# Planning the landing of every transfer a fifth later in a list scheduler

## The chip, the core and the metric

One core of a Trainium2 chip runs the whole program. The metric is the device time of one execution in microseconds (us). PE is TensorE (matrix products), DVE is VectorE, ACT is ScalarE, POOL is GpSimd, SP is SyncE, which here only issues transfers (DMAs). Each engine works through its own instructions in their order; an instruction that needs another engine's result waits on a semaphore, and all behind it on its engine wait too.

## The reference

A decoder trunk of two layers on 1024 tokens of width 1024, all in fp32. The first layer mixes tokens by a causal convolution, the second by sliding-window attention; an MLP with a squared ReLU and a gated embedding (p) follow in each.

```
def conformer_conv(x, w_in, b_in, w_dw, b_dw, ln_g, ln_b, w_out, b_out):
    a, gate = jnp.split(x @ w_in + b_in, 2, axis=-1)
    h = a * jax.nn.sigmoid(gate)
    h = causal_depthwise_conv(h, w_dw, width=31) + b_dw
    h = jax.nn.silu(layer_norm(h, ln_g, ln_b))
    return h @ w_out + b_out

for i in range(2):
    y = conformer_conv(x, ...) if i == 0 else swa_sink_attention(x, ...)   # window 128, 16 heads, 4 kv heads
    x = layer_norm(ALPHA * x + y)
    x = layer_norm(ALPHA * x + square(relu(x @ w_up)) @ w_down)
    x = x + (p[i] @ ple_w_proj[i]) * sigmoid(x @ ple_w_gate[i])
```

## The kernel before

Every fp32 product is made of three products on PE: operands are split in a high part and the rest (tiles xh and xl for activations, wh and wl for weights), and xh\*wh, xl\*wh and xh\*wl are summed in PSUM. A 128x1024 block of weights is loaded into a raw tile, ACT casts it to wh, DVE subtracts to get wl.

The program goes through: the products of w_in with the sigmoid gate (conv_in), the convolution as banded products (taps, ps<-B,E, whose operand B is stored to DRAM as scr and loaded back shifted), the norm and Silu (conv_ln), w_out (mix_out), the MLP, the gated embedding (PLE), K and V, attention, and MLP and PLE again. Each stage is emitted by a function of Emit, in the order of a plain program, with a generator for some that are to fill others' waits. embed(0) is such a filler: p times w_proj, eight products per half (each of six matmuls), copied from PSUM by ACT into a t tile and stored to DRAM (proj<-t).

Nothing of that order is final. The Recorder (lines 200 to 470) keeps every operation with its tiles and its dependences; schedule() (line 321) plays the program through once with estimated durations (cost(), line 291) and so fixes, for each of the five engines, the order in which its instructions are issued (issue(), line 459, whose line 469 shows for each instruction of the profile). In that play, an operation becomes ready when the last thing that it needs has its planned end. The engine that is free first takes the ready operation with the lowest priority number, which is its place in the plain program, moved by later(). finish() (line 367) sets an operation's planned end, and with it the ready times of what needs it and the times at which the buffers it used last come free.

Buffers count as much as data: tiles are given out from slots by tag. There are 6 of ps (a PSUM bank) and 2 of tr (two banks for transposes; one of ps is moved to tr once the convolution is through), 5 each of t, wh and wl, 2 of raw, 9 of B. A tile waits until a slot is free, and then waits in reality for the last user of that slot.

For a transfer the plan (lines 449 to 452) keeps SP busy 380 ns, adds its size over the bandwidth to a running queue (dma), and ends it at that queue's time or 2800 ns after issue, whichever is later. In the program that is issued, SP runs the transfers in the planned order, and each of them also waits on one of eight semaphores used in turn (DMAHW0 to 7), so for the landing of the transfer issued eight before it.

In conv_ln, for two rows of blocks at a time, DVE takes the statistics (sm), POOL turns them into factors with a power and scales the tiles X and A, PE transposes them, ACT applies Silu into a t tile, ACT or DVE casts it to xh and DVE subtracts to xl. DVE's SCALAR_TENSOR_TENSOR on sm stands between two steps of POOL.

Of the kernel before, what the change touches and what calls it, by code (L numbers as in the profile page):

```python
# [45 lines left out]
SC = 144  # L46
ROWS = slice(0, P // 2), slice(P // 2, P)
WAIT = 250.0
MIX_GROUPS = (
    ((0, 1, 2, 3), (4, 5, 6, 7)), ((0, 1), (2, 3), (4, 5), (6, 7)),  # L50
)
# [148 lines left out]
class Recorder:  # L200
# [120 lines left out]
    def schedule(self):  # L321
# [11 lines left out]
        def both(o):  # L333
            if o.eng == "gpsimd":
                return o.name != "memset" and o.outv[0].n > 8
            if o.eng != "vector":
                return False
            if o.name == "tensor_copy":
                src = o.allv
            else:  # L340
                src = [v for k, v in o.kw.items() if k in ("in0", "in1") and isinstance(v, View)]
            return len(src) > 1 and not any(v.buf.space == "PSUM" for v in src)
# [5 lines left out]
        dma = 0.0  # L348
# [4 lines left out]
        def delay(o, x):  # L353
            a, b = o.eng, x.eng
            if a in ("alloc", "sync") or b == "alloc":
                return 0.0
            if a == b:
                return same.get(a, 0.0)
            return 200.0 if a == "tensor" else 260.0 if b == "tensor" else 150.0

        def enable(o):
            if o.eng == "alloc":
                return
            for e in ("vector", "gpsimd") if o.eng == "either" else (o.eng,):
                heapq.heappush(fut[e], (o.ready, o.prio, o.num, o))

        def finish(o, end):
            o.end = end
            order.append(o)
            for x in o.outs:  # L370
                r = end + delay(o, x) + (0.0 if o.eng in ("tensor", "alloc") else x.slack)
                if r > x.ready:
                    x.ready = r
                x.left -= 1
                if x.left == 0:
                    enable(x)
            for b in o.bufs:
                b.users -= 1
                b.end = max(b.end, end)
                if b.users == 0 and b.slot is not None:  # L380
                    heapq.heappush(self.tags[b.tag]["free"], (b.end + lat, b.slot))
                    serve(b.tag)

        def serve(tag):
            t = self.tags[tag]
            q = t["queue"]
            while q and t["free"]:
                o = q.pop(0)
                ft, s = heapq.heappop(t["free"])
                o.alloc.slot = s  # L390
                if o.name == "move":
                    dst = o.args[1]
                    heapq.heappush(self.tags[dst]["free"], (ft, s))
                    finish(o, ft)
                    serve(dst)
                else:
                    finish(o, ft)
# [9 lines left out]
        while True:  # L407
            best = None
            for e in engs:
                while rdy[e] and rdy[e][0][2].end:  # L410
                    heapq.heappop(rdy[e])
                while fut[e] and fut[e][0][3].end:
                    heapq.heappop(fut[e])
                if rdy[e]:
                    t = free[e]
                elif fut[e]:
                    t = max(free[e], fut[e][0][0])
                else:
                    continue
                if best is None or t < best[0]:  # L420
                    best = (t, e)
            if best is None:
                break
            t, e = best
            while fut[e] and fut[e][0][0] <= t:
                r, p, i, o = heapq.heappop(fut[e])
                if not o.end:
                    heapq.heappush(rdy[e], (p, i, o))
            p, i, o = heapq.heappop(rdy[e])
            if WAIT and fut[e] and e != "tensor":  # L430
                r, p2, i2, o2 = fut[e][0]
                if not o2.end and r <= t + WAIT and p2 < p - 300:
                    heapq.heappush(rdy[e], (p, i, o))
                    heapq.heappop(fut[e])
                    t, o = r, o2
            if o.eng == "either":
                o.eng = e
                o.dur = self.cost(o, o.outv, o.allv)
            d = o.dur
            if e == "scalar" and o.name == "activation":  # L440
                k = TABLE.get(o.args[2].name if len(o.args) > 2 else "", 0)
                if k and k != table:
                    table = k
                    d += 1283.0
            if both(o):
                d += max(0.0, held["gpsimd" if e == "vector" else "vector"] - 50.0 - t)
                held[e] = t + d
            free[e] = t + d
            if e == "sync":
                v = o.allv[0]  # L450
                dma = max(dma, t + 1400.0) + v.n * v.parts / 75.0
                finish(o, max(dma, t + 2800.0))
            else:
                finish(o, t + d)
        assert len(order) == len(self.ops), (len(order), len(self.ops))
# [46 lines left out]
class Emit:  # L502
# [563 lines left out]
    def mix_out(self, i, w, gb, tiles, lhs=None):  # L1066
# [4 lines left out]
        for cc in range(2):  # L1071
            us = ws.get(4)
            for g in MIX_GROUPS[cc]:
                pss = self.tok_group(g, us, lhs, last=g is MIX_GROUPS[cc][-1])
                if cc == 0:
                    nc.slack = WORK_SLACK * i
                    for k in MIX_WORK[i][g is MIX_GROUPS[cc][-1]]:
                        self.up_ahead(i, k, "At"[i])
# [917 lines left out]
```

## Time and profile before

| | us |
|---|---|
| median of 3 runs | 2141.74 |
| lowest and highest | 2140.77, 2145.20 |
| profiled execution, whole | 2140.78 |
| its span (first to last instruction) | 2139.1 |
| mean granted clock of PE | 0.999 |

The span is what the profile's rows cover; 1.7 us of the execution lie around it. A row of a timeline gives the start in the span, the duration, the engine, and in brackets the idle time of that engine just before and what ended it. A row of busy time by stretch gives the stretch, its length, PE's busy time with the number of matmuls, the granted clock, the share of the DMA engines' time in use and GB/s. The first embed products stand near 245 us, w_out begins at 292, the first layer's PLE ends about 1080 and attention about 1390.

### The profile page before, as it was taken

To read this page: it belongs to the slowest core of one execution; us is meant where nothing else is said; L and a number is where in the kernel's file an instruction comes from. 1 tells how busy PE (TensorE), PEld (TensorE's weight loads), DVE (VectorE), ACT (ScalarE), POOL (GpSimd) and SP (SyncE) were. 2 spreads that over 40 slices of the span, in tenths; PEclk is the share of its full clock that TensorE was granted. 3 is DMA by queue.
4 is the path that set the end of the run, shared out by engine and by line. 5 is a ranking of instruction groups with operands and counts; after the bars stand their busy time and mean duration, and the time that the engine had idled before them with its cause. 6 is when DMAs were issued, how large, how long until landed. Compare 5 with 4: busy or idle time off the path is not lost.

```text
span 2139.1 us, 29650 instructions
## 1 busy us (share of the span) xinstructions
PE 2118.0 (99%) x9940; PEld 1748.0 (82%) x9940; DVE 1736.6 (81%) x2823; ACT 1144.6 (54%) x2162; POOL 285.7 (13%) x530
## 2 busy tenths in 40 slices
PE   9999999999999999999999999999999999999999
PEld 7888778888888888888788878888888888888877
DVE  6566678898898888876986888689988988788688
ACT  5455673554544633335755888455445554333484
POOL 0000042300000000001310666250000000000042
PEclk9999999999999999999999999999999999999999
DMA  8654664747787856655487022665778785565726
GB/s 256 174 151 142 198 217 159 249 151 257 268 278 266 302 175 208 204 180 211 161 281 252 14 87 80 214 229 190 258 262 294 263 332 173 180 233 170 263 72 233
DMA packets 209928, 443.16 MB, mean 207 GB/s; under 512 B 21744, under 2 KB 57200, under 8 KB 209776
## 3 DMA queue, kind: packets, MB, share of 16 engines
q1 hardware_dynamic: 209776, 441.27, 62.2%
q8 instruction: 78, 1.28, 0.2%
q14 instruction: 74, 0.61, 0.1%
HBM read 296.75 MB, written 144.44 MB: 206 GB/s over the span
## 4 chain that ended last, share of the span: by engine, by line
PE 45%; ACT 2%; DVE 2%; DMA 2%; issue 1%; POOL 0%; SPq 0%; DVEq 0%; ACTq 0%; POOLq 0%
PE ps L469 31%; PE tr L469 14%; ACT z L469 1%; DMA raw<-in_w_kv_dram 0%; ACT wh L469 0%; ACT xh L469 0%; DVE t L469 0%; DMA raw<-form 0%; POOL sm L469 0%; DMA raw<-gate_t 0%; DVE B L469 0%; ACT t L469 0%; DVE z L469 0%; DMA raw<-in_w_q_dram 0%; DMA B<-xsp 0%
## 5 line engine op out<-in xcount | busy, mean ns | idle before, releaser
L469 PE MATMUL ps<-xh 128*128 128x512 f32 x618 | 240.4, 389 | 0.0
L469 PE MATMUL ps<-xl,xh 128*128 128x512 f32 x618 | 240.4, 389 | 0.0
L469 PE MATMUL ps<-xh,xl 128*128 128x512 f32 x618 | 240.4, 389 | 0.0
L469 ACT CAST wh<-raw 128x1024 fp32r<-128x1024 f32 (+2 forms) x158 | 148.2, 941 | 154.9 <-PE ps L469 90.5
L469 PE MATMUL ps<-xl,wh 128*128 128x512 f32 x540 | 210.9, 391 | 0.3 <-DVE xl L469 0.3
L469 PE MATMUL ps<-xh,wl 128*128 128x512 f32 x540 | 210.6, 390 | 0.0
L469 PE MATMUL ps<-xh,wh 128*128 128x512 f32 x540 | 209.3, 392 | 0.4 <-ACT xh L469 0.4
L469 POOL TENSOR_SCALAR sm<-sm 128x1 f32<-128x1 f32 x72 | 25.8, 362 | 1363.7 <-DVE E L469 600.8
L469 PE MATMUL ps<-wh,xh 128*128 128x512 f32 x392 | 154.6, 395 | 2.5 <-DVE t L469 1.5
L469 PE MATMUL ps<-wl,xh 128*128 128x512 f32 x392 | 155.0, 395 | 0.0
L469 PE MATMUL ps<-wh,xl 128*128 128x512 f32 x392 | 154.7, 395 | 0.0
L469 ACT CAST xh<-wh 128x1024 fp32r<-128x1024 f32 x76 | 79.9, 1051 | 116.5 <-PE ps L469 90.3
L469 ACT CAST wh<-g 128x512 fp32r<-128x512 f32 x108 | 65.1, 621 | 140.0 <-DVE g L469 56.2
L469 PEld LDWEIGHTS ps<-xh,xl 128*128 128x128 f32 x618 | 116.0, 188 | 24.3
L469 PEld LDWEIGHTS ps<-xh 128*128 128x128 f32 x618 | 116.0, 188 | 24.0
L469 PEld LDWEIGHTS ps<-xl,xh 128*128 128x128 f32 x618 | 116.0, 188 | 23.9
L469 DVE TENSOR_TENSOR wl<-raw,wh 128x1024 fp32r<-128x1024 f32 (+1 forms) x102 | 103.9, 1020 | 36.1 <-ACT wh L469 34.8
L469 PEld LDWEIGHTS ps<-xh,wh 128*128 128x128 f32 x540 | 101.7, 188 | 22.1 <-ACT xh L469 0.8
L469 PEld LDWEIGHTS ps<-xl,wh 128*128 128x128 f32 x540 | 101.6, 188 | 20.7 <-DVE xl L469 1.4
L469 PEld LDWEIGHTS ps<-xh,wl 128*128 128x128 f32 x540 | 101.4, 188 | 20.6
L469 DVE TENSOR_TENSOR xl<-wh,xh 128x1024 fp32r<-128x1024 f32 x76 | 93.0, 1223 | 24.3 <-ACT xh L469 24.3
L469 DVE TENSOR_TENSOR E<-z,cst 128x832 fp32r<-128x832 f32 x64 | 64.0, 1021 | 57.9 <-PE ps L469 57.9
(425 smaller groups left out, 5642.1 us busy)
## 6 DMA issues: line engine op xcount, KB each, us to landing
wh<-hid SPq DMA_DIRECT2D x78, 512.0 KB, 4.4
raw<-in_w_up_dram SPq DMA_DIRECT2D x61, 512.0 KB, 4.3
wl<-in_w_down_dram SPq DMA_DIRECT2D x58, 512.0 KB, 4.7
hid<-zz SPq DMA_DIRECT2D x96, 256.0 KB, 3.4
hid<-t SPq DMA_DIRECT2D x70, 256.0 KB, 3.0
raw<-hid SPq DMA_DIRECT2D x30, 512.0 KB, 3.8
scr<-zz SPq DMA_DIRECT2D x32, 256.0 KB, 3.7
B<-scr SPq DMA_DIRECT2D x64, 128.0 KB, 4.0
```

The source lines that it names most:

```text
L469: getattr(getattr(nc, o.eng), o.name)(*a, **k)
```

## The change

One constant is added, and every transfer's planned landing is set 600 ns later by it. How long SP is planned to be busy with a transfer, how transfers share the bandwidth (dma) and all costs of the other engines stay as they are. No operation is added or removed.

```
 WAIT = 250.0
+LAND = 600.0
...
             if e == "sync":
                 v = o.allv[0]
                 dma = max(dma, t + 1400.0) + v.n * v.parts / 75.0
-                finish(o, max(dma, t + 2800.0))
+                finish(o, max(dma, t + 2800.0) + LAND)
             else:
                 finish(o, t + d)
```

So a lone small transfer is planned to land 3400 ns after issue instead of 2800, and everything that a landing makes ready, a consumer or the next user of a slot that a store had read, is taken up later in the play. What was ready at the time is taken in its stead, and the orders of all five engines differ from there on, in part only by which slot a tile has. The rows below are the order in which an engine issues (a number behind a tile's name is its slot, the longer ones only tell tiles apart; the wait behind a row names the semaphores).

**The start.** PE before, at the first banded product (ps<-B,E):

```order
L469 MATMUL ps5_363_687<-xl00_244_308,wh4_7_71 128x512
L469 MATMUL ps5_363_687<-xh00_243_307,wl4_12_76 128x512
L469 MATMUL ps5_363_687<-xh10_247_311,wh0_348_595 128x512 [waits Activation_49]
L469 MATMUL ps5_363_687<-xl10_248_312,wh0_348_595 128x512
L469 MATMUL ps3_357_661<-B1_24_88,E0_40_104 128x256 [waits DMAHW4_49,Pool_49]
L469 MATMUL ps3_357_661<-B1_24_88,E0_40_104 128x256
```

and now, where the same product is the last row but one:

```order
L470 MATMUL ps5_363_687<-xh10_247_311,wl0_348_596 128x512
L470 MATMUL ps5_363_687<-xh10_247_311,wh0_347_593 128x512
L470 MATMUL ps5_363_687<-xl10_248_312,wh0_347_593 128x512
L470 MATMUL ps5_363_687<-xh10_247_311,wl0_348_596 128x512
L470 MATMUL ps0_367_723<-xh00_243_307,wh4_7_71 128x512 [waits DVE_49]
L470 MATMUL ps0_367_723<-xl00_244_308,wh4_7_71 128x512
L470 MATMUL ps0_367_723<-xh00_243_307,wl4_12_76 128x512
L470 MATMUL ps0_367_723<-xh00_243_307,wh4_7_71 128x512
L470 MATMUL ps0_367_723<-xl00_244_308,wh4_7_71 128x512
L470 MATMUL ps3_358_666<-B1_24_88,E0_40_104 128x256 [waits DMAHW5_49,DMAHW4_49,Pool_49]
L470 MATMUL ps3_358_666<-B1_24_88,E0_40_104 128x256
```

Ten rows of input products stand here between xl10,wh0 and B1, with five more above them: 15 matmuls more than before stand ahead of B1.

**The first embed products, about 248 us.** PE before, where the products for tile ps2_608 begin and the taps on B3 follow:

```order
L469 MATMUL ps2_602_2630<-wh2_540_2168,wl3_546_2195 128x512
L469 MATMUL ps2_608_2671<-wh2_540_2168,wh1_511_1907 128x512 [waits Activation_49]
L469 MATMUL ps2_608_2671<-wl2_541_2170,wh1_511_1907 128x512
L469 MATMUL ps4_593_2570<-B3_584_2498,E0_40_104 128x256 [waits DMAHW7_49,Pool_49]
L469 MATMUL ps4_593_2570<-B3_584_2498,E0_40_104 128x256
```

and now, where the other six matmuls of ps2_608 and a group of four transposes stand above these rows:

```order
L470 MATMUL ps1_609_2673<-wh2_540_2168,wh1_511_1907 128x512 [waits PE_49]
L470 MATMUL ps1_609_2673<-wl2_541_2170,wh1_511_1907 128x512
L470 MATMUL ps1_609_2673<-wh2_540_2168,wl1_512_1910 128x512
L470 MATMUL ps1_609_2673<-wh2_540_2168,wh3_545_2192 128x512
L470 MATMUL ps1_609_2673<-wl2_541_2170,wh3_545_2192 128x512
L470 MATMUL ps0_593_2570<-B3_584_2498,E0_40_104 128x256 [waits DMAHW1_49,DMAHW0_49,Pool_49]
L470 MATMUL ps0_593_2570<-B3_584_2498,E0_40_104 128x256
```

The two matmuls between ps2_602's last and B3 have become eleven and four transposes. SP before, in the run of loads for these taps:

```order
L469 DMA B4_586_2511<-scr7_109_173 128x2x256
L469 DMA B7_594_2573<-scr7_109_173 64x2x256 [waits DMAHW4_49,Pool_49]
L469 DMA B6_588_2543<-scr7_109_173 128x2x256
L469 DMA B0_600_2609<-scr7_109_173 64x2x256 [waits DMAHW6_49,Pool_49]
L469 DMA B3_584_2498<-scr7_109_173 64x2x256 [waits DMAHW7_49]
L469 DMA proj0_2_86_150<-t0_566_2359 128x512 [waits DMAHW0_49,Activation_49]
L469 DMA B8_596_2583<-scr7_109_173 128x2x256 [waits DMAHW1_49]
```

and now:

```order
L470 DMA B4_586_2511<-scr7_109_173 128x2x256
L470 DMA B7_594_2573<-scr7_109_173 64x2x256 [waits DMAHW4_49,Pool_49]
L470 DMA B6_588_2543<-scr7_109_173 128x2x256
L470 DMA B0_600_2608<-scr7_109_173 64x2x256 [waits DMAHW6_49,Pool_49]
L470 DMA proj0_2_86_150<-t0_566_2359 128x512 [waits DMAHW7_49,Activation_49]
L470 DMA B8_596_2583<-scr7_109_173 128x2x256 [waits DMAHW0_49]
L470 DMA B3_584_2498<-scr7_109_173 64x2x256 [waits DMAHW1_49]
L470 DMA g0_603_2632<-in_mix_g_dram 128x512 [waits DMAHW2_49,DVE_49,PE_49]
```

The second half of B3 (the lower of the two B3 loads of this stretch) stood right behind B0; now the store proj0_2 and the load B8 stand between.

**Between the norm and w_out, about 290 us.** ACT before, from the copy for which PE waits at 290.93 us (t1_700<-ps0_680) to the copy that frees slot 4 of ps (t0_693<-ps4_677):

```order
L469 ACTIVATE t4_690_3077<-tr0_695_3107,cst_240_304 128x256 [waits DMAHW0_49,PE_49]
L469 COPY t1_700_3125<-ps0_680_3030 128x512 [waits DVE_49]
L469 ACTIVATE t4_690_3077<-tr0_695_3107,cst_240_304 128x256
L469 COPY t0_693_3088<-ps4_677_3020 128x512 [waits DMAHW2_49]
L469 CAST xh10_247_311<-t4_690_3077 128x2x256 [waits Activation_49]
```

and now, from the copy of the same kind (t1_698<-ps5_681), to the copy that frees slot 2 (t0_692<-ps2_669), in two pieces; first:

```order
L470 COPY t1_698_3118<-ps5_681_3043 128x512 [waits DVE_49,PE_49,Activation_49]
L470 CAST xh00_243_307<-t2_682_3047 128x2x256 [waits Activation_49]
L470 ACTIVATE t3_684_3058<-tr1_657_2950,cst_240_304 128x256 [waits DMAHW0_49]
L470 ACTIVATE t3_684_3058<-tr1_657_2950,cst_240_304 128x256
L470 ACTIVATE t4_687_3069<-ps0_694_3101,cst_240_304 128x256 [waits DMAHW1_49,PE_49]
L470 CAST wh0_705_3140<-raw1_680_3041 128x1024 [waits DMAHW7_49,PE_49]
L470 ACTIVATE t4_687_3069<-ps0_694_3101,cst_240_304 128x256
```

and, six rows of Silu and xh casts further:

```order
L470 ACTIVATE t3_717_3177<-ps0_716_3169,cst_240_304 128x256 [waits DVE_49,PE_49]
L470 ACTIVATE t4_718_3180<-tr1_719_3182,cst_240_304 128x256 [waits DVE_49,PE_49]
L470 ACTIVATE t3_717_3177<-ps0_716_3169,cst_240_304 128x256
L470 ACTIVATE t4_718_3180<-tr1_719_3182,cst_240_304 128x256
L470 COPY t0_692_3089<-ps2_669_2987 128x512 [waits DMAHW2_49]
```

Before, the second copy was two rows behind the first, and now it is 17: 12 Silu pieces, three xh casts and a wh cast stand between. PE before, from the product that waits for the first copy to the first one of w_out (ps4_712):

```order
L469 MATMUL ps0_707_3148<-wh2_636_2833,wh0_578_2467 128x512 [waits Activation_49]
L469 MATMUL ps0_707_3148<-wl2_634_2828,wh0_578_2467 128x512
L469 MATMUL ps0_707_3148<-wh2_636_2833,wl0_579_2470 128x512
L469 MATMUL tr0_709_3152<-ident_241_305,A2_16_80 128x128 [waits PE_49,Activation_49]
L469 MATMUL tr0_709_3152<-ident_241_305,A3_17_81 128x128 [waits Pool_49]
L469 MATMUL tr0_709_3152<-ident_241_305,A2_16_80 128x128
L469 MATMUL tr0_709_3152<-ident_241_305,A3_17_81 128x128
L469 MATMUL ps4_712_3159<-wh3_670_3002,xh00_243_307 128x512 [waits DVE_49,Activation_49]
L469 MATMUL ps4_712_3159<-wl4_671_3003,xh00_243_307 128x512
```

and now, from the product that waits for the first copy to the first of w_out (ps2_729); first the product:

```order
L470 MATMUL ps5_701_3126<-wh2_625_2784,wh0_578_2467 128x512 [waits Activation_49]
L470 MATMUL ps5_701_3126<-wl2_623_2780,wh0_578_2467 128x512
L470 MATMUL ps5_701_3126<-wh2_625_2784,wl0_579_2470 128x512
L470 MATMUL ps5_701_3126<-wh2_625_2784,wh1_658_2954 128x512
L470 MATMUL ps5_701_3126<-wl2_623_2780,wh1_658_2954 128x512
L470 MATMUL ps5_701_3126<-wh2_625_2784,wl1_660_2958 128x512
```

and, five groups of four transposes further, the sixth and w_out's first product:

```order
L470 MATMUL tr1_727_3210<-ident_241_305,A4_18_82 128x128 [waits PE_49,Activation_49]
L470 MATMUL tr1_727_3210<-ident_241_305,A5_19_83 128x128 [waits Pool_49]
L470 MATMUL tr1_727_3210<-ident_241_305,A4_18_82 128x128
L470 MATMUL tr1_727_3210<-ident_241_305,A5_19_83 128x128
L470 MATMUL ps2_729_3217<-wh3_663_2967,xh00_243_307 128x512 [waits DVE_49,Activation_49]
L470 MATMUL ps2_729_3217<-wl4_664_2968,xh00_243_307 128x512
```

The first product of w_out takes slot 2 of ps, which the second copy frees, behind six matmuls of embed and 24 transposes; before, it took slot 4 behind three matmuls and four transposes. On DVE, in the same stretch, the subtraction for wl1 now stands ahead of six statistics rows that it followed, and the cast xh and the subtraction xl for the first Silu piece stand ahead of the last one or two SCALAR_TENSOR_TENSOR rows on sm instead of behind them.

More of the change, by code (lines that the diff above doesn't have):

```diff
@@ L48 @@
 WAIT = 250.0
+LAND = 600.0
 MIX_GROUPS = (
@@ L451, in schedule @@
                 dma = max(dma, t + 1400.0) + v.n * v.parts / 75.0
-                finish(o, max(dma, t + 2800.0))
+                finish(o, max(dma, t + 2800.0) + LAND)
             else:
```

## The prediction

> **What bounds the kernel now.** First the page's busy times, then the waits of PE, then PE's busy time by stretch of the span.
>
> ```profile
> span 2139.1 us, 29650 instructions
> PE 2118.0 (99%) x9940; PEld 1748.0 (82%) x9940; DVE 1736.6 (81%) x2823; ACT 1144.6 (54%) x2162; POOL 285.7 (13%) x530
> ...
> PE ps L469 <- ACT t L469: 4.0, 2, 2.7
> PE ps L469 <- DVE t L469: 3.9, 5, 1.5
> PE ps L469 <- DMA B<-scr: 2.6, 2, 1.9
> ...
> 240.00:300.00 60.00, 54.02 (x289) 0.97 0.86 265
> ...
> 500.00:600.00 100.00, 100.00 (x442) 1.00 0.80 266
> 1080.00:1390.00 310.00, 307.04 (x1610) 1.00 0.47 157
> 1390.00:2020.00 630.00, 629.93 (x2808) 1.00 0.70 237
> ```
>
> PE (TensorE) is busy 2118.0 of 2139.1 us. So no order of the same work, at an unchanged clock, gains more than the 21.1 us in which PE stands, and every new microsecond of PE idle is lost whole. A stretch with no idle gives the price of one 128x512 product: 100.00 / 442 = 0.226 us of PE. The waits row by row (tile waited for, total, times, longest) say that transfers end only 2.6 us of PE's waiting on a large scale, in two waits for B<-scr; ACT and DVE end most of the rest. The idle is local: 240 to 300 us holds 60.00 - 54.02 = 6.0 us of it, 1080 to 1390 holds 3.0, and 1390 to 2020 next to nothing.
>
> **The change part by part.** It moves a planned number, so the question is what the plan had wrong and where the new order differs. The plan gave a lone transfer 2.8 us and a 512 KB one 1.4 + 1.75 = 3.15 us; now 3.4 and 3.75. Measured (KB each, median us to landing):
>
> ```profile
> wl<-in_w_down_dram SPq DMA_DIRECT2D x58, 512.0 KB, 4.7
> ...
> B<-scr SPq DMA_DIRECT2D x64, 128.0 KB, 4.0
> ```
>
> The new figure is nearer to the chip, and still short by 0.6 to 1.0 us. That alone buys nothing where no wait for a transfer ends on PE's path. The Trainium skill, "DMA: Bandwidth & Descriptors", section "Anatomy of one DMA", gives a fit of about 2.0 us plus bytes over 436 GB/s, some 3.2 us for 512 KB: by it the old plan was right and the new one only holds consumers and slots back. The 4.7 us row disagrees, so the sum does not use it.
>
> PE's order of products is the same through the two MLPs and the end of the program. It differs in four places.
>
> *Start (to 55 us).* In the new order 15 more input products stand ahead of the first product on B: 15 x 0.226 = 3.4 us of work, in front of this wait:
>
> ```profile
> 54.92 1.32 PE L469 MATMUL ps<-B,E 128*128 128x256 f32 x9 [0.75 <-DMA B<-scr]
> ```
>
> The 0.75 us goes: **-0.75** (0 if that load, which SP now issues behind one more transfer, is late by as much).
>
> *The first embed products (247 to 256 us).*
>
> ```profile
> 248.31 0.50 PE L469 MATMUL ps<-wh,wh 128*128 128x512 f32 x1 [1.24 <-ACT t L469]
> 248.65 0.40 PE L469 MATMUL ps<-wl,wh 128*128 128x512 f32 x1
> 250.92 1.13 PE L469 MATMUL ps<-B,E 128*128 128x256 f32 x7 [1.88 <-DMA B<-scr]
> ...
> 251.00:252.00 1.00, 1.00 (x8) 0.91 1.08 278
> 252.00:255.00 3.00, 3.00 (x15) 0.50 1.05 301
> 255.00:256.00 1.00, 1.00 (x10) 0.89 0.93 280
> ...
> 291.00:292.00 1.00, 1.00 (x6) 1.00 0.28 106
> ...
> 241.75 4.80 SPq L469 DMA_DIRECT2D B<-scr  x7
> 246.64 0.55 SPq L469 DMA_DIRECT2D proj<-t  x1
> 247.24 1.05 SPq L469 DMA_DIRECT2D B<-scr  x2
> ```
>
> The wait of 1.24 us for a copy stays: the same ACT work stands ahead of it. Behind it two products ran before, and now eleven and a group of four transposes: 11 x 0.226 + 0.44 = 2.9 us from 248.31, to 251.2 (0.44 is the step between two groups of transposes, 287.16 to 287.60 below). The load waited for does not come sooner: the second half of B3 was the last of the run of seven loads, and now stands behind a store and another load, at the place of the pair at 247.24. I take it as 1.1 us later, 252.0. So the gap is 0.75 instead of 1.88: **-1.1** (-1.9 if the load keeps its time, 0 if it is 1.1 us later still). The two gaps with 0.5 us of work between them also cost clock: from 251 to 256 the granted clock was 0.91, then 0.50 for 3 us, then 0.89, or 0.09 + 1.5 + 0.11 = 1.7 us of PE at full speed. With 2.9 us of work between the gaps I expect that dip to go: **-1.7** (0 if not). A single gap of 2.73 us ahead of 290.93 (below) cost no clock.
>
> The Trainium skill, "TensorE: Matmul & The Clock Gate", section "What's actually happening", has the clock halve after an idle window of about 3.4 us and come back after as long a busy one. Both rows agree with that: about 4 us nearly idle gave 0.50, 2.73 us gave none. By that rule each new gap above 3.4 us would cost about 1.7 us of clock besides.
>
> *The convolution's normalization and the first w_out products (270 to 300 us).*
>
> ```profile
> 276.65 0.16 DVE L469 SCALAR_TENSOR_TENSOR sm<-sm,sm 128x1 f32<-128x1 f32 x1 [0.30 <-POOL sm L469]
> ...
> 277.84 1.21 DVE L469 TENSOR_TENSOR wl<-raw,wh 128x1024 fp32r<-128x1024 f32 x1
> ...
> 288.23 0.16 DVE L469 SCALAR_TENSOR_TENSOR sm<-sm,sm 128x1 f32<-128x1 f32 x1 [3.98 <-POOL sm L469]
> ...
> 288.82 0.42 DVE L469 CAST xh<-t 128x512 fp32r<-128x512 f32 x1
> 289.27 0.98 DVE L469 TENSOR_TENSOR xl<-t,xh 128x512 fp32r<-128x512 f32 x1
> ...
> 290.29 0.59 ACT L469 COPY t<-ps 128x512 f32<-128x512 f32 x1 [2.36 <-DVE xl L469]
> 290.77 0.57 ACT L469 ACTIVATE t<-tr,cst 128x256 f32<-128x256 f32 x1
> 291.23 0.59 ACT L469 COPY t<-ps 128x512 f32<-128x512 f32 x1
> 291.70 0.64 ACT L469 CAST xh<-t 128x512 fp32r<-128x512 f32 x1
> 292.22 0.59 ACT L469 ACTIVATE t<-ps,cst 128x256 f32<-128x256 f32 x1
> 292.68 1.06 ACT L469 CAST wh<-raw 128x1024 fp32r<-128x1024 f32 x1
> 293.63 0.58 ACT L469 ACTIVATE t<-ps,cst 128x256 f32<-128x256 f32 x1
> ...
> 287.16 0.60 PE L469 MATMUL ps<-ident,X 128*128 128x128 f32 x4
> 287.60 0.60 PE L469 MATMUL tr<-ident,X 128*128 128x128 f32 x4
> 290.93 0.50 PE L469 MATMUL ps<-wh,wh 128*128 128x512 f32 x1 [2.73 <-ACT t L469]
> ...
> 292.08 0.48 PE L469 MATMUL ps<-wh,xh 128*128 128x512 f32 x1
> ```
>
> Before, a product of embed waits 2.73 us for an ACT copy; that copy waits for DVE's xl, and DVE for POOL's chain of statistics. The chain starts when PE has transposed the last tap. Those transposes now stand 11 products later, 11 x 0.226 = 2.5, which the 1.1 and the 1.7 us saved above cancel: -0.3. (That is all that those two savings do, so they stand in the sum through this chain alone.) The 1.2 us wl now runs ahead of statistics and costs what is not covered by DVE's wait of 0.30, some 0.8 us; the casts xh (0.42, and its neighbour) move ahead of the last two statistics and give 0.96 back (288.23 to 289.27, less 0.08 for the one small instruction left). The copy therefore comes at 290.29 - 0.3 + 0.8 - 0.96 = 289.8, and PE's product at about 290.4, half a microsecond earlier with half a microsecond less work done: no gain or loss there, though its gap grows.
>
> Then comes the new stall. Before, three products and four transposes later (292.08) the first w_out product runs, since its PSUM slot was freed by the ACT copy two rows behind the one waited for (291.23). Now that slot is freed by a copy 17 rows behind. Between them stand 12 Silu pieces, three xh casts and a wh cast. Starts of successive rows give 0.46, 0.52 and 0.95 for each (290.77 to 291.23, 291.70 to 292.22, 292.68 to 293.63) and 0.48 for the first copy: 0.48 + 12 x 0.46 + 3 x 0.52 + 0.95 = 8.5 us, and 0.59 for the copy itself. So w_out starts at 289.8 + 8.5 + 0.6 + 0.1 = 299.0. PE has 6 products and 24 transposes until then, 6 x 0.226 + 6 x 0.44 = 4.0 us, and stands idle for 299.0 - 290.4 - 4.0 = 4.6 us. PE had no idle behind 293 to win it back from. **+4.6** (2.6 if the copy at 289.8 comes 2 us sooner, 6.2 if the clock dip above stays). Whether ACT's seventeen rows wait for transposes can only lengthen it.
>
> I add **+0.8** for clock, half of one dip, since the gap ahead of 290.4 would be near 5 us and is followed by waiting anyway, and the second is 4.6 (bounds 0 and two dips, 3.4).
>
> *End of the first PLE to the end of attention (1080 to 1390 us).* Everything is re-dealt at a fine grain, with PE at 307.04 of 310. Its gaps are small, for DVE and ACT:
>
> ```profile
> 1095.87 0.66 PE L469 MATMUL ps<-ident,B 128*128 128x128 f32 x4 [0.62 <-DVE xl L469]
> ...
> 1242.53 0.70 PE L469 MATMUL ps<-A,v 128*128 128x512 f32 x2 [0.80 <-DVE t L469]
> ```
>
> The most to be gained is 3.0 us; as much can be lost. With transposes in whole groups of four and the first score products closer behind theirs I take **+0.3**.
>
> Sum: -0.75 + 4.6 + 0.8 + 0.3 = +4.95 on the profiled execution's 2140.78 us (its span is 1.7 us less), 2145.7. The three runs have their median at 2141.74, 0.96 above that execution: **2146.7 us**.
>
> **Rivals.** *A wait is filled and nothing takes its place (faster).* Place: the copies on ACT behind 289.8. If the slot of the first w_out product is in truth free when PE comes (the 17 rows run ahead of PE by 4.6 us or more, that is, the copy starts by 285.2), the stall is nothing, and 0.75 + 1.1 + 1.7 + most of 2.73 are won: about -5.5, or 2136.2. For it: the new order takes the casts ahead of the last statistics. Against it: DVE's 3.98 us wait for POOL stands ahead of xl in both orders, and POOL's chain is not shortened.
>
> *It is the same within 0.2% (4.28 us, about what a measurement of this kernel can tell from no change).* PE's order is unchanged over most of the span and only 21.1 us are idle in all; with a stall of 2.6 instead of 4.6 and no clock lost the sum is -0.75 + 2.6 + 0.3 = +2.2, or 2143.9.
>
> *Both new gaps cost clock.* Then +4.95 - 0.8 + 3.4 = +7.55, or 2149.3. The row for it is the 0.50 at 252; the row against it is the 1.00 at 291 behind 2.73 us.
>
> *The change does not do what it says.* No transfer is quicker or slower for it; were the order the same the time would be 2141.7. The order does differ, so this has no share.
>
> **How the numbers follow.** Forecast (one stall, no more than one dip) 0.37; both dips 0.15; no measurable difference 0.35; faster 0.13. So slower by over 0.2% 0.52, within 0.35, faster 0.13. The likeliest case is a loss of about 5 us. The range reaches down to 2137.5, into the faster rival so that only its better half is left out, and up to 2152.5: 2149.3 with 3 us lost in attention as well.
>
> **What would show it.** Right: no gap ahead of the first product on B near 55 us; clock 1.00 from 250 to 256; PE idle for 4 to 5 us ahead of the first w_out product near 299, waiting for an ACT copy; 300 to 1080 as before, shifted by about 4. Wrong: a w_out product that starts before 295; a first-half loss that is won back before 1080; or a change of more than 3 us between 1080 and 1390, which I priced at nearly nothing.

## The result and the profile after

| | before | after |
|---|---|---|
| median | 2142.3 us (4 runs) | 2153.05 us (4 runs) |
| lowest and highest of after | | 2152.44, 2153.6 |
| ratio after / before, 95% interval | | 1.0052 [1.004, 1.0064] |
| span of the profiled execution | 2139.1 us | 2151.9 us |
| PE busy | 2118.0 us | 2122.7 us |

It is slower by 10.75 us in the medians and by 12.8 us between the two profiled executions. The forecast was 2146.7 with a range up to 2152.5: the sign was right, the size less than half, and the range did not hold the time.

One warning for all that follows. A profile is one execution, and timed runs of the kernel before lie between 2138.6 and 2145.8 us. A kernel whose order is the same up to 1900 us (the run e11_tail below) had its row of 2070.83 at 2071.88, so differences below about 1 us at one place mean nothing. A profiled execution can also lie off the median of its own kernel: 3.4 us above it in e5_early, 2.8 below in e7_proj, 2.6 below in e10_ahead.

The page of after, and PE's waits there (tile waited for, total, times, longest):

```profile
span 2151.9 us, 29625 instructions
PE 2122.7 (99%) x9940; PEld 1751.9 (81%) x9940; DVE 1740.4 (81%) x2821; ACT 1145.3 (53%) x2162; POOL 285.1 (13%) x532
...
PE ps L470 <- ACT t L470: 5.8, 4, 3.9
PE ps L470 <- DMA B<-scr: 5.7, 3, 4.0
```

PE runs the same 9940 matmuls, yet is busy 4.7 us longer, and stands 29.2 us (2151.9 - 2122.7) where it stood 21.1. The first goes with a slower clock (the mean granted clock is 0.996, it was 0.999), the second is waits: B<-scr was 2.6 us and is 5.7, and its longest is 4.0 instead of 1.9.

Now the same places as in the prediction, PE's rows in order of time (idle before a row and its releaser in brackets):

```profile
57.74 1.67 PE L470 MATMUL ps<-B,E 128*128 128x256 f32 x12 [1.15 <-DMA B<-scr]
...
247.97 0.50 PE L470 MATMUL ps<-wh,wh 128*128 128x512 f32 x1 [1.25 <-ACT t L470]
...
255.26 2.83 PE L470 MATMUL ps<-B,E 128*128 128x256 f32 x12 [4.04 <-DMA B<-scr]
...
293.91 0.80 PE L470 MATMUL ps<-wh,wh 128*128 128x512 f32 x1 [3.86 <-ACT t L470]
...
299.78 1.11 PE L470 MATMUL tr<-ident,A 128*128 128x128 f32 x4 [1.23 <-ACT t L470]
...
302.12 1.12 PE L470 MATMUL ps<-ident,X 128*128 128x128 f32 x4 [0.38 <-ACT t L470]
...
303.74 0.78 PE L470 MATMUL ps<-wh,xh 128*128 128x512 f32 x1
...
1032.57 0.63 PE L470 MATMUL ps<-ident,E 128*128 128x128 f32 x4 [0.46 <-DVE E L470]
...
1765.43 0.50 PE L470 MATMUL tr<-xh 128*128 128x512 f32 x1 [1.66 <-ACT xh L470]
...
2082.14 0.50 PE L470 MATMUL ps<-wh,xh 128*128 128x512 f32 x1 [0.64 <-DVE t L470]
...
2133.53 0.50 PE L470 MATMUL ps<-wh,xh 128*128 128x512 f32 x1 [1.57 <-DVE v L470]
```

Against the rows of before (248.31, 250.92, 290.93, 292.08, then these, which were not shown yet):

```profile
1022.95 0.63 PE L469 MATMUL ps<-ident,E 128*128 128x128 f32 x4 [0.49 <-DVE E L469]
...
2070.83 0.50 PE L469 MATMUL ps<-wh,xh 128*128 128x512 f32 x1 [0.71 <-DVE t L469]
```

the 12.8 us divide so: -0.34 up to the wait at 248; then 1032.57 - 247.97 = 784.60 against 1022.95 - 248.31 = 774.64, or **+9.96**; then 1049.57 against 1047.88, +1.69; and +1.5 behind 2070.83. The first of these stretches is measured for every experiment below; its excess over 774.64 is called **lag**.

PE's busy time and clock by stretch (stretch, length, busy with matmuls, granted clock, DMA share, GB/s) show where the lag arises:

```profile
250.00:255.00 5.00, 1.22 (x6) 1.00 0.86 268
255.00:256.00 1.00, 0.74 (x4) 0.67 0.97 255
256.00:258.00 2.00, 2.00 (x11) 0.50 0.93 311
258.00:260.00 2.00, 2.00 (x13) 0.81 0.85 259
290.00:294.00 4.00, 0.14 (x2) 0.86 0.23 70
294.00:300.00 6.00, 4.77 (x15) 0.50 0.42 131
300.00:306.00 6.00, 5.62 (x21) 0.50 0.64 213
306.00:308.00 2.00, 2.00 (x11) 0.87 0.43 161
...
320.00:1080.00 760.00, 757.62 (x3398) 1.00 0.65 217
1080.00:1390.00 310.00, 307.50 (x1613) 1.00 0.45 151
1390.00:2020.00 630.00, 628.03 (x2798) 1.00 0.69 235
```

The whole lag arises between 250 and 308; from 320 to 1390 nothing is lost. The gaps there grew from 1.24 + 1.88 + 2.73 = 5.9 us to 1.25 + 4.04 + 3.86 + 1.23 + 0.38 = 10.8, so 4.9. The clock gives the rest: behind 255 the dip is as large as before (0.33 x 0.74 + 0.5 x 2 + 0.19 x 2 = 1.6 us), and a second one, from 294 to 307, is new: half of 4.77 + 5.62, and 0.13 x 2, or 5.5 us. Together 10.3, for a lag of 9.96.

### The profile page after: what moved, and what is told of

Its sections match the earlier page's. It is cut to its first block, busy times and chain, and to the rows that moved or that the text cites. A ratio compares the mean times of both kernels' runs of the same rounds, so it can differ in the third digit from the quotient of the medians.

```text
span 2151.9 us, 29625 instructions
## 1 busy us (share of the span) xinstructions
PE 2122.7 (99%) x9940; PEld 1751.9 (81%) x9940; DVE 1740.4 (81%) x2821; ACT 1145.3 (53%) x2162; POOL 285.1 (13%) x532
## 4 chain that ended last, share of the span: by engine, by line
PE 45%; ACT 3%; DVE 2%; DMA 1%; issue 1%; POOL 0%; ACTq 0%; DVEq 0%; POOLq 0%
PE ps L470 33%; PE tr L470 12%; ACT z L470 1%; DMA t<-proj 1%; ACT xh L470 0%; DVE t L470 0%; POOL sm L470 0%; DVE B L470 0%; DMA raw<-gate_t 0%; ACT t L470 0%; DVE z L470 0%; DVE A L470 0%; ACT bo L470 0%; DVE sm L470 0%; DVE zz L470 0%
## 5 line engine op out<-in xcount | busy, mean ns | idle before, releaser
L470 PE MATMUL ps<-xl,xh 128*128 128x512 f32 x636 | 247.4, 389 | 0.0
L470 PE MATMUL ps<-xh,xl 128*128 128x512 f32 x636 | 247.4, 389 | 0.0
L470 PE MATMUL ps<-xh 128*128 128x512 f32 x636 | 246.6, 389 | 0.0
L470 PE MATMUL ps<-xl,wh 128*128 128x512 f32 x564 | 220.3, 391 | 0.0
L470 PE MATMUL ps<-xh,wl 128*128 128x512 f32 x564 | 220.0, 390 | 0.0
L470 PE MATMUL ps<-xh,wh 128*128 128x512 f32 x564 | 218.5, 391 | 0.0
L470 PE MATMUL ps<-wh,xh 128*128 128x512 f32 x412 | 162.7, 395 | 2.6 <-DVE v L470 1.6
L470 PE MATMUL ps<-wh,xl 128*128 128x512 f32 x412 | 163.3, 396 | 0.0
L470 PE MATMUL ps<-wl,xh 128*128 128x512 f32 x412 | 163.0, 396 | 0.0
L470 PEld LDWEIGHTS ps<-xh,wl 128*128 128x128 f32 x564 | 105.9, 188 | 21.6
```

Source lines behind the costliest of these rows:

```text
L470: getattr(getattr(nc, o.eng), o.name)(*a, **k)
```

## The experiments

Most experiments change the kernel after by moving single instructions in the planned order, so that data and dependences stay and the engines' queues alone differ. All use this hook, each with its own list of (instruction, the instruction that it is put behind):

```
-            for o in self.schedule():
+            order = self.schedule()
+            for n, m in MOVES:
+                o = next(x for x in order if x.num == n)
+                order.remove(o)
+                order.insert(1 + next(i for i, x in enumerate(order) if x.num == m), o)
+            for o in order:
```

### SP's order as before (e1_swap)

The store proj_1 goes behind B3's first load, the store proj_2 and the load B8 behind B3's second. Nothing else moves.

```
+MOVES = [(2420, 2443), (2430, 2444), (2572, 2430)]
```

> The changed kernel, with three transfers put back on SP: the store proj_1 behind the first B3 load, the store proj_2 and the load B8 behind the second B3 load, as they stood before the change. Theory A (the loss begins with these loads: the gap of 4.04 us ahead of the first taps on B3, the clock dip behind it, and the late chain of the norm): the gap falls to 0.3 to 1.4 us, the clock is 1.00 from 256 us on, the product that waits near 293.9 starts at 289 to 290.5, the whole is 4 to 6.5 us shorter than the changed kernel, about 2148. Theory B (the loss is the ACT copy that stands 17 rows late, whatever the loads do): the gap near 251 shrinks but the first w_out product still starts 4 us or more behind the product that waits for its copy and idle moves there; under 2 us gained, about 2151.5.

Measured: 2150.45 us, ratio 1.0039 [1.0023, 1.0054], span 2148.3, lag 6.62. PE's rows in order of time:

```profile
250.96 1.59 PE L476 MATMUL ps<-B,E 128*128 128x256 f32 x12
...
255.19 3.43 PE L476 MATMUL ps<-B,E 128*128 128x256 f32 x26 [1.48 <-DMA B<-scr]
...
289.95 0.80 PE L476 MATMUL ps<-wh,wh 128*128 128x512 f32 x1 [3.86 <-ACT t L476]
...
299.78 0.78 PE L476 MATMUL ps<-wh,xh 128*128 128x512 f32 x1
```

and PE by stretch:

```profile
250.00:255.00 5.00, 3.71 (x22) 1.00 0.96 290
...
289.00:302.00 13.00, 10.45 (x35) 0.50 0.48 156
```

With the loads back the taps on B3 follow their eleven products without a gap at 250.96 (forecast 251.2), the clock dip is gone, and w_out starts at 299.78 (forecast 299.0). A later load (B8) is waited for instead, 1.48 us. So three places in SP's queue carry 3.3 us of the lag, and the other 6.6 us stand without them. The 13 us at half clock from 289 stay as they were. In the medians the gain is 2.6 us, or 1.9 when each kernel is set against the kernel before that was timed beside it. Theory A asked for 4 to 6.5 and theory B for under 2: each has its place right and neither has the sum. One of the four runs took 2144.59 us, at a mean clock of 0.999 where the other three had 0.996 or 0.997.

### The two gaps filled (e2_fill)

Sixteen additional products in front of the taps on B3 and eight repeats of a group of transposes in front of the product that waits at 293.91; their results are overwritten or repeat what is there.

```
+FILL_AT = {2448: [again(2448, 2618, 16)], 3001: [redo((2869, 2870, 2871, 2872), 8)]}
...
             for o in self.schedule():
...
+                for f in FILL_AT.get(o.num, ()):
+                    f(self, nc)
                 getattr(getattr(nc, o.eng), o.name)(*a, **k)
```

> The changed kernel with PE kept busy in its two long gaps: 16 more products of 128x512 ahead of the first taps on B3, into the PSUM tile that the taps then start anew, and 8 more repeats of a group of four transposes ahead of the product that waits near 293.9. Nothing waits for less. Theory C (the half clock behind a long gap costs several us of its own): clock 1.00 from 256 to 260 and from 294 to 307, and the whole 3 to 5 us shorter, about 2149. If the clock is only a sign of the gaps and PE is waiting anyway: within 1 us of the changed kernel, about 2153.

Measured: 2149.17 us, ratio 1.0040 [1.0026, 1.0053], lag 6.79. PE by stretch:

```profile
247.00:255.00 8.00, 6.85 (x32) 1.00 1.04 267
...
294.00:300.00 6.00, 2.75 (x17) 0.83 0.35 108
300.00:310.00 10.00, 10.00 (x45) 0.76 0.60 217
```

Work that computes nothing saves 3.2 us of lag and 3.9 in the medians, as theory C had it: PE waits as long for its data, but at full clock behind it. It saves nothing at the second place: PE comes sooner through its transposes and then waits for ACT in gaps of 1.20, 1.23 and 0.82 us, so w_out starts at 301.29 and the clock sinks there. Behind 290 ACT's queue sets the time up to w_out's start, whether PE passes it waiting or at half clock.

### The copy for w_out early (e3_wout) and both repairs (e9_both)

e3_wout puts the copy that frees w_out's PSUM slot two rows behind the first copy, as before, and six w_out products ahead of five groups of transposes. e9_both does this and the moves of e1_swap.

```
+MOVES = [(2834, 2804), (3146, 2834), (3150, 2882), (3151, 3150), (3152, 3151), (3153, 3152), (3154, 3153), (3155, 3154)]
```

> The changed kernel, with the ACT copy that frees the slot of the first w_out product moved to two rows behind the copy that PE waits for, as before the change, and the first six w_out products moved ahead of five of the six groups of transposes. Theory B (this place costs the 4.6 us of the prediction): w_out starts before 299 and the whole is 3 to 5 us shorter, about 2149. Theory A (PE's wait there is 1.2 and 0.4 us, the rest is the late start of the chain and the clock): 0.5 to 2 us shorter, about 2152.

> The changed kernel with the two loads of B3 ahead of proj_1, proj_2 and B8 again (as in e1_swap) and with the early copy and the early w_out products (as in e3_wout). Lag is the time from the wait at 248 to the rows near 1023, less the 774.6 us that it was before; the changed kernel has 9.96, e1_swap 6.62, e3_wout 7.97. Theory 1 (the late load and the late copy are two separate losses, the product of both is small): lag 9.96 - 3.3 - 2.0 = 4.6, median about 2148. Theory 2 (they multiply, since a clock dip behind the second gap needs both): lag below 3.5, median below 2146.5, clock of 0.9 or more from 290 to 310.

Measured: e3_wout 2151.7 us, ratio 1.0050 [1.0034, 1.0067], lag 7.97; w_out starts at 297.95. e9_both 2147.69 us, 1.0025 [1.0015, 1.0035], lag 6.45. Of the 2.0 us by which e3_wout lags less than after, 0.8 are not its own: its taps on B3 stand 6.48 us behind the wait at 248 (7.29 in after), ahead of all that was moved. So the early copy is worth about 1.2 us, as theory A had it, and the intervals of e3_wout and after overlap. PE's rows in e9_both:

```profile
289.38 0.79 PE L476 MATMUL ps<-wh,wh 128*128 128x512 f32 x1 [3.91 <-ACT t L476]
...
612.53 0.73 PE L476 MATMUL tr<-X,wh 128*128 128x512 f32 x2 [1.72 <-ACT t L476]
```

and PE by stretch:

```profile
290.00:294.00 4.00, 4.00 (x13) 0.50 0.59 197
294.00:300.00 6.00, 4.43 (x29) 0.96 0.46 97
```

In e9_both the lag contains three waits for ACT in the MLP that the kernels before and after do not have there (0.35 near 593, 1.72 near 613, 0.26 near 617; why the moves bring them was not tried). Without these 2.3 us it is 4.1, near the 4.6 of two separate losses; with them it lies above both theories. The medians do not decide either: each set against the kernel before timed beside it, the two moves gain 1.9 and 0.6 us alone and 4.2 together, and each median has an interval of some 2 to 3.5 us either way. That the losses add is therefore likely and not shown. What both repairs leave in the lag is the gap of 3.91 us ahead of 289.38 (before, 2.73), the half clock behind it, which lasted until 294.5 and cost some 2.5 us, and waits of 1.09 and 0.48 us for ACT at 297.59 and 299.19. No run takes these away.

### Only the late transfers (e4_late), only the last (e11_tail)

```
-                finish(o, max(dma, t + 2800.0) + LAND)
+                finish(o, max(dma, t + 2800.0) + (LAND if t >= FROM else 0.0))
```

with FROM at 320000 ns of the plan in e4_late and at 1900000 in e11_tail.

> The later landing from the planned time 320 us on only; up to there every engine has the order of before. Theory A (what counts happens before 320 us): the lag behind the kernel of before is 0 at 1000 us and the end has the 3 us of the rest (near 1760 and in the last 20 us): about 2145. If the loss is spread over the program: 2147 or more. If the later landing helps where transfers are waited for: under 2141.

> The 600 ns are added only to transfers planned from 1900 us on (e4_late: from 320 on, which left a gap of 1.65 us at 1755 and one of 1.04 at 2123, some 1.9 us in all). Theory 1 (two separate places): the rows up to 1800 as before, without a gap at 1755, and a gap of about 1 us between 2115 and 2135, end about 0.5 to 1.3 us later than before. Theory 2 (the tail's loss follows from the order at 1755): no gap in the tail, the end within 0.3 us of before.

Measured: e4_late 2143.27 us, ratio 1.0007 [0.9998, 1.0016], span 2141.0, lag -0.2. Its PE shows the two late gaps of after and no other new one (the half clock behind 291 is in the last section):

```profile
1754.77 0.50 PE L471 MATMUL ps<-xh 128*128 128x512 f32 x1 [1.65 <-ACT xh L471]
...
2122.76 0.50 PE L471 MATMUL tr<-wh,xh 128*128 128x512 f32 x1 [1.04 <-DVE v L471]
```

e11_tail: 2142.2 us, 1.0001 [0.9992, 1.001], without either gap, and 68.4 us from its row at 2071.88 to the end, against 68.3 before. So what after loses behind 1390 (1.9 us of PE's time up to 2020, and 1.5 in the tail) comes with transfers planned between 320 and 1900; in e4_late's spans it is 1.9 us, and its interval reaches from nothing to 3.4. Which of the transfers it is stays open. The plans of e11_tail and after have the same order on all five engines from the planned time 2000 us on, and only the slots that the tiles get differ; so the gap in the tail does not come from the order there. In after, DVE waits 2.27 us for t<-proj at 2130.13, just ahead of the last gap; that names the load, not why it is late.

### Only the early transfers, and of these one kind (e5_early, e6_scr, e7_proj)

The added time holds for all transfers planned before 320 us (FROM as in e4_late); of these for the stores to scr and the loads of B alone; for the stores of proj alone.

```
-                finish(o, max(dma, t + 2800.0) + LAND)
+                finish(o, max(dma, t + 2800.0) + (LAND if t < FROM else 0.0))
...
+                finish(o, max(dma, t + 2800.0) + (LAND if (v.buf.tag.startswith('scr') or v.buf.tag == 'B') and t < 320000.0 else 0.0))
...
+                finish(o, max(dma, t + 2800.0) + (LAND if v.buf.tag.startswith('proj') and t < 320000.0 else 0.0))
```

> The later landing for all transfers, up to the planned time 320 us alone. If what stands behind 320 us is independent: lag of 9.6 us at 1023 as in the changed kernel and nothing more behind it, about 2151. If the two parts add (theory A and B both hold): its lag equals the sum of the lags of the run with scr and B alone and the run with proj alone, within 1 us; if they multiply, it is 3 us or more above that sum.

> The later landing for the convolution's transfers alone (stores of scr and loads of B), and up to the planned time 320 us alone; everything else as before the change. On SP the B3 loads stand behind proj stores as in the changed kernel; on ACT and PE the copy and the first w_out product stand about where they did before. Theory A (the SP order is the loss): gap of about 4 us ahead of the taps near 255, half clock behind it, and a lag of 5 to 7 us behind the kernel of before at the E transposes near 1023; about 2148. Theory B (the w_out place is the loss, the loads only delay what waits anyway): lag of 2 to 3.5 us at 1023, about 2145.

> The later landing for the stores of proj alone, up to the planned time 320 us alone; the rest as before. SP's order up to 250 us is that of before; on ACT the copy that frees the slot of the first w_out product stands six rows behind the first copy instead of two, on PE seven matmuls later. Theory A: lag at 1023 within 1 us of the kernel of before, about 2142. Theory B (a copy k rows later costs those ACT rows, 0.46 to 0.5 us each): lag of 1.5 to 3 us, about 2144.

| | median us | ratio | lag us | gap at the taps on B3 | first w_out product |
|---|---|---|---|---|---|
| e5_early | 2148.42 | 1.0030 [1.0018, 1.0041] | 10.33 | 3.56 | 304.61 |
| e6_scr | 2145.74 | 1.0017 [1.0008, 1.0027] | 4.72 | 2.95 | 292.00 |
| e7_proj | 2144.59 | 1.0009 [0.9999, 1.0018] | 1.77 | 1.71 | 292.07 |

The landing of scr and B alone makes the late load and its clock dip (0.78 and 0.54 from 250 to 260), with w_out in its old place; the lag of 4.72 lies between the two theories. The landing of proj alone does neither: the clock is 1.00 throughout and only small waits for ACT come in (1.73 us at 286.42), as theory B had it. The late slot of w_out appears only when both are planned later. Whether this costs more than the two alone stays open. The traces say so (10.33 against 4.72 + 1.77 = 6.5), but the medians do not: above the kernel before timed beside them (2142.06), e5_early is 6.4 us longer and the other two 3.7 and 2.5, together 6.2. The trace of e5_early is that of the longest of its seven runs. Behind its row at 1034.28 e5_early takes 1115.8 us, against 1116.2 before, and has neither of the two late gaps, so what stands behind 320 us is independent.

### Twice the added time (e8_l1200)

```
-LAND = 600.0
+LAND = 1200.0
```

> The constant doubled, 1200 ns for all transfers (a 512 KB load is then planned at 4.35 us, about what is measured). If a landing nearer to the measured one is better by itself: at or under the kernel of before, 2142 or less, and under the changed kernel by 5 us or more at any rate. If more delay of the same kind costs more: over 2155. If each value deals another order and the time is the luck of a few places (theory D): anywhere between 2139 and 2153, not between the two others in any order, and its gaps near 250 and 290 us tell which: on PE w_out's first product stands where it stood before.

Measured: 2144.43 us, ratio 1.0012 [1.0003, 1.0021], lag 2.78. PE by stretch:

```profile
250.00:255.00 5.00, 5.00 (x25) 1.00 0.97 317
...
290.00:294.00 4.00, 2.94 (x7) 0.55 0.34 130
```

Twice the change costs a quarter of it. The first place is better than before the change: PE works through from 250 to 255 at full clock, where it had a gap and a dip. Behind the second gap (3.73 us ahead of 291.06) the clock is lost for some microseconds, and w_out starts at 293.78, near its old place. So the time does not follow the planned landing: what counts is what falls into these two places.

### The gap filled in the kernel before (e10_ahead, e12_ahead2)

Eight embed products are moved ahead of the taps on B3 in the kernel before; in e12_ahead2 four input products ahead of the first product on B at 54.92 as well.

```
+MOVES = [(2559, 2558), (2560, 2559), (2561, 2560), (2562, 2561), (2618, 2562), (2619, 2618), (2620, 2619), (2621, 2620)]
```

> The kernel before, with eight embed products moved ahead of the taps on B3 at 250.9 us and nothing else (1.8 us of work into the gap of 1.88). Theory 1 (a gap filled with work that has to be done anyway, and a clock dip avoided, are won, since all behind depends on the last tap): gap gone, clock 1.00 from 250 to 256, lag (as in e9_both) between -1.8 and -3.5, median 0.1 per cent below before. Theory 2 (the next load, B7 or B8, is waited for in its stead, and from 290 on PE waits for ACT anyway): clock 1.00 but a new gap above 1 us near 253 to 256, lag between -1 and 0, no difference that can be measured.

> e10_ahead with four input products moved ahead of the first product on B at 54.9 us as well (0.9 us of work into the gap of 0.75 us); nothing else differs from the kernel before. In e10_ahead the trace was 2.8 us shorter between 248 and 1023, the timed runs the same within 0.1 per cent. Theory 1 (both fills are won): no gap near 55, the wait at 248 about 0.7 us sooner, lag (as in e9_both) -2 to -3, median 0.1 to 0.17 per cent below before, interval below 1. Theory 2 (what was won in e10_ahead's one profiled execution is mostly the spread from run to run, some microseconds): interval of the ratio around 1, within 0.1 per cent either way.

Measured: e10_ahead 2141.29 us beside 2141.17, ratio 0.9998 [0.999, 1.0007]; e12_ahead2 2140.66 beside 2141.26, 0.9998 [0.9989, 1.0007]. PE in e10_ahead from 250 to 255, and the row of its next gap:

```profile
250.00:255.00 5.00, 5.00 (x34) 1.00 1.06 298
```

```profile
258.80 1.92 PE L475 MATMUL ps<-B,E 128*128 128x256 f32 x14 [1.26 <-ACT B L475]
```

The gap of 1.88 us and the dip are gone, and a wait of 1.26 us for ACT stands in their place at 258.80. The profiled execution had a lag of -2.82, that of e12_ahead2 of -0.3, with a new wait of 0.93 us near 606. The timed runs allow at most 2.1 and 2.4 us of gain, and show none. No version was found that is measurably faster than the kernel before.

## Why the prediction was wrong

Between the two profiled executions it forecast +4.95 us and +12.8 came, so 7.9 are missing: 0.4 at the start, 4.6 in the lag, where +5.4 was forecast, 1.4 from there to 2082, and 1.5 in the tail. By its own steps:

- **The start (-0.75): not as told.** The gap ahead of the first product on B is not gone; it stands at 57.74 with 1.15 us, since the load lands 2.8 us later and PE comes only 2.4 us later: of the 3.4 us of additional products, it does a part in time in which it stood before (51.76 us busy up to 54 before, 52.49 now). That the wait at 248 is 0.34 us sooner lies within the spread.
- **The first embed products (-1.1 and -1.7, carried as -0.3 in the chain): this step failed.** It took B3's second load to stand "at the place of the pair at 247.24", and so 1.1 us later, landing at 252.0. SP after (start, duration, count), and its loads of B issued from 241 to 249 as a group, with their times to landing:

```profile
241.42 6.11 SPq L470 DMA_DIRECT2D B<-scr  x7
...
248.21 1.06 SPq L470 DMA_DIRECT2D B<-scr  x2
```

```profile
L470 SPq DMA_DIRECT2D B<-scr x9: 426/586/1370, 241.4 to 248.7; - x9
...
DMA to landing us min/median/max: 4.0/4.7/6.4
```

  Of the pair B8 is the first; B3's load is the second and is issued at 248.7, the last start of the group. And the run of seven takes SP 6.11 us instead of 4.80, so all behind it is later. Before, the load was the last of a run that ended at 246.55, so issued near 246.0: it is now 2.7 us later, of which the forecast had the 1.1, the second place in the pair is 0.5, and the longer run 1.0. PE's row comes 6.5 us behind it, at 255.26 (before, 4.9, at 250.92), and the DMA engines were busy 0.86 to 0.97 of that time; why the load takes 1.6 us longer was not tried. The gap is 4.04 instead of 0.75, and the clock dip, taken as gone, is as large as before. The way on was as forecast: every later step runs through the last tap, the copy on ACT comes at 293.27 instead of 289.8, and the waiting product at 293.91 instead of 290.4. The upper bound that the step gave ("0 if it is 1.1 us later still") was too near for the same reason. e1_swap undoes just this and has the copy at 289.31, near the 289.8 of the forecast.
- **The stall at w_out (+4.6): right in place, cause and, with its cover, in size.** ACT after, first and last of the stretch:

```profile
293.27 0.59 ACT L470 COPY t<-ps 128x512 f32<-128x512 f32 x1 [5.89 <-DVE sm L470]
...
302.38 0.62 ACT L470 COPY t<-ps 128x512 f32<-128x512 f32 x1
```

  The seventeen rows take 9.1 us (forecast 8.5; 0.57 us of it is one wait for transposes), and 9.1 us in e1_swap too.
- **The clock (+0.8): mis-sized, and split wrongly.** The second dip is 5.5 us, not 0.8. But PE idles at w_out only 1.23 + 0.38 us, not 4.6: at half clock its 24 transposes and six products fill most of what was forecast as idle. The two terms together, 5.4, stand against e1_swap's lag of 6.62 (5.9 without a wait of 0.68 us for ACT near 613 that before does not have), so their sum was near by luck. In after a part of the dip reaches past w_out's start to 307. The two rows that the prediction weighed, 2.73 us without a dip and two short gaps with one, do not bound what a gap costs: behind a single gap of 2.65 us the clock halved in e4_late, whose order is the same up to there, and two gaps of 1.24 and 1.71 us left it at 1.00 in e7_proj (the last section says why).
- **Attention (+0.3): nothing there.** PE is busy 307.50 of 310 us between 1080 and 1390, 307.04 before; and 757.62 of 760 between 320 and 1080 with 757.58 before.
- **The rest (no term): this step failed too.** The 1.9 us near 1760 and the 1.5 us in the tail had no term, because PE's order was taken as the same "through the two MLPs and the end of the program". The two plans differ at 2240 of PE's 9940 places, in 14 stretches and not in four. Most of them cost nothing. One is at 1757 to 1765 in after: there PE goes to and fro between the products of four tiles, which before, at 1748 to 1757, it took six by six, and it waits 1.66 us for a cast to xh. In the tail eight products change places; e11_tail has the same order there and no gap, so what brings that gap stays open.

Of the rivals, "both new gaps cost clock" came nearest (2149.3); it kept the first gap closed and so still lacked the late load. The Trainium skill's rule, "TensorE: Matmul & The Clock Gate", section "What's actually happening" (half clock after an idle window of about 3.4 us), agrees with the gaps of 4.04 and 3.86 us, which both gave 0.50. The prediction weighed it against gaps that it had forecast as 0.75 and 4.6. In one point the traces differ from that rule, and they decide: the window need not be idle throughout, since up to 1.57 us of work in 3.41 went with a halved clock (last section). The fit that the prediction took from the Trainium skill, "DMA: Bandwidth & Descriptors", section "Anatomy of one DMA", is given there for transfers issued from GpSimd. SP issues all of these, so the 4.7 us row does not speak against it.

## What to carry to other kernels

A list scheduler's estimate that comes nearer to the truth need not give a better program: here 600 ns on every transfer cost 0.5%, 1200 ns 0.12%, and the 600 ns on parts of the transfers between 0.01 and 0.3%, depending mostly on what fell ahead of two waits. When a queue's order changes, find the one place where PE stands for that queue, and count every instruction in front of it, the last of a merged row included, with the time of the whole queue shifted. A gap of some 2 to 4 us on PE is to be priced with the clock behind it, and below 3.7 us that price is a matter of chance: a single trace with or without a dip does not settle it.

## What the runs showed of the hardware

- The granted clock changes only on a fixed grid of 3.41 us. The times follow from its mean over 1 us: in after it is 0.67 from 255 to 256, so it fell from 1 to 0.5 at 255.34. It rose at 258.74, fell at 292.88 and rose at 306.54; these lie 1, 11 and 15 steps of 3.413 us behind the first. The other traces fit the same step (before: 251.82 and 255.22; e4_late: 250.38, 253.80, 291.34 and 294.76; e6_scr: 252.78, 259.60, 297.16 and 300.56). Half clock lasted one, two or four steps. Where the grid lies differs from execution to execution: before, e4_late and e11_tail have the same order up to 320 us, and the clock fell at 251.82, 250.38 and 252.32.
- What counts is how long PE was busy in the step that ends. In the 14 traces, between 243 and 311 us, the clock halved behind each of the 16 steps at full clock with at most 1.57 us of work, and behind none with 1.76 or more. It came back behind each of the 16 steps at half clock with 2.97 us of work or more, and behind none of the 14 with 2.96 or less. In after the waits of 1.23 and 0.38 us left 2.39, 2.25 and 2.96 us in three steps, which is why half clock lasted four; in e9_both the second step was full, and it lasted two.
- So the same gap costs clock or not by where it falls. The gap near 290, then PE by stretch behind it, in e4_late; and the same stretch in before (gap 2.73) and e11_tail (2.72):

```profile
290.31 0.50 PE L471 MATMUL ps<-wh,wh 128*128 128x512 f32 x1 [2.65 <-ACT t L471]
...
290.00:294.00 4.00, 3.69 (x13) 0.67 0.73 166
```

```profile
290.00:294.00 4.00, 3.07 (x15) 1.00 0.57 126
```

```profile
290.00:294.00 4.00, 2.89 (x15) 1.00 0.52 110
```

  An estimate from the figures above: a single gap within unbroken work costs no clock below about 1.6 us (3.41 - 1.76) and always does above about 3.7 (twice 3.41 - 1.57). All gaps of 3.73 to 4.04 us did.
- A load of 128 KB, 4.0 us in the median over the kernel before, took 6.4 us in after from 248.7 on, where the DMA engines were 0.9 busy.
